# First product of each feed-forward by seven products of quarters instead of eight, and rms with positions on partitions

## Chip, cores and metric

The kernel runs on one core of one Trainium2 chip. What is measured is the device time of one execution in microseconds (us); several executions are timed and the median is given. One more execution is taken with the hardware profiler, and all rows below come from it. The core's engines each have a queue of their own, worked off in order: TensorE (PE; its weight loads PEld), VectorE (DVE), ScalarE (ACT), GpSimd (POOL), and SyncE (SP), which here issues the transfers. Matmuls write into eight accumulator banks (PSUM); all other tiles lie in the on-chip memory SBUF.

## The reference

A decoder trunk of two layers, 512 positions, width 1024, in float32. Layer 0 mixes by an RWKV recurrence, layer 1 by dilated attention, both with attention to a memory of 256 rows beside it. Ahead of and behind each mixer stands a feed-forward at half weight, so there are four: 00, 01, 10, 11.

```python
def swiglu_ffn(x, norm_g, w_in, w_out):
    gate, up = jnp.split(rms_norm(x, norm_g) @ w_in, 2, axis=-1)
    return (jax.nn.silu(gate) * up) @ w_out
...
        x = x + 0.5 * swiglu_ffn(x, ffn_pre_norm[layer], ffn_pre_w_in[layer], ffn_pre_w_out[layer])
```

`w_in` is 1024 x 5632 (2816 columns of gate, 2816 of up), `w_out` 2816 x 1024.

## The kernel before

Activations are kept transposed: features on the 128 partitions, the 512 positions along the free axis, so a state is 8 tiles of 128x512. Products run in a rounded float32 format (`fp32r`) with both factors split into a high part and the rest, and three matmuls for each 128x128 weight tile: high by high, high by low, low by high (`dense`). A weight comes in pieces of up to four tiles (128x512, 256 KB). For each piece `weight` issues the transfer into `raw` on SyncE's queue, copies it to the high part `whi` on ScalarE, and subtracts for the low part `wlo` on VectorE or GpSimd in turn. There are six `raw` slots and four each of `whi` and `wlo`.

In `ffn`, the operand u (parts `uh`, `ul`) is the state by the gain; the factor 1/rms (`rstd`) is applied after the product, since it belongs to the position. For each of the 22 column blocks m, the gate and the up product (8 tiles of k, 24 matmuls of 512 columns each) fill two of the eight banks `fps`. VectorE takes the gate by rstd (`gs`), ScalarE makes the Silu, VectorE multiplies it by up (`hm`), and this is split into `hh` on ScalarE and `hl` on VectorE. The second product goes over the 22 hidden blocks for each of the 8 output blocks j; `add_state` adds it to the old state, which is fetched again (`xin`), and forms the next operand.

Operand.rstd sums the squares over partitions with a matrix of ones, 128x512 wide, and takes root and reciprocal of all 128x512 equal rows. The memory's operand, the bias rows of the dilated attention (`bias_rows`, by way of DRAM) and the reload of the state for the shared keys and values run as side steps within the first products; the memory's keys and values (`memory_kv`) come behind 00, and within 01 at its last column block.

The order on each engine is made by the framework's scheduler from the order of the code; the slots of the pools (`take`) set when a tile can be filled again. All operations of the engines are recorded by one helper and so show line L278 in the profile; groups are told apart by tile names.

## Time and profile before

| | |
|---|---|
| three timed executions | 2134.22, 2135.74, 2138.95 us; median 2135.74 |
| profiled execution | 2133.36 us |
| its span, first to last instruction | 2131.6 us |
| mean granted TensorE clock | 0.995 of full speed |

By stage, in us from the start of the span: feed-forward 00 from 6 to 373, the memory's keys and values 373 to 386, first mixer to 805, feed-forward 01 to 1185, feed-forward 10 to 1546, second mixer to 1766, feed-forward 11 to the end. Of these, by busy time:

| stage | length | TensorE | VectorE | ScalarE | GpSimd |
|---|---|---|---|---|---|
| feed-forward 00 | 367 | 364.42 | 141.71 | 140.42 | 86.71 |
| first mixer | 419 | 379.59 | 270.42 | 159.86 | 150.80 |
| feed-forward 01 | 380 | 379.81 | 155.46 | 142.04 | 94.28 |
| feed-forward 10 | 361 | 360.59 | 131.78 | 128.89 | 86.61 |
| second mixer | 220 | 208.46 | 155.00 | 118.42 | 66.82 |
| feed-forward 11 | 365 | 359.52 | 120.83 | 116.69 | 89.24 |

A row of the profile that stands for a group gives engine, operation, written tile <- read tiles, shapes, the count, then busy time in us and the mean of one in ns, and behind it the idle time of its engine just before these instructions, with what ended it. A row of the timeline gives start and duration in us of a single instruction (x2: two of them run together).

### The profile page before, as it was taken

To read this page: it belongs to the slowest core of one execution; us is meant where nothing else is said; L and a number is where in the kernel's file an instruction comes from. 1 tells how busy PE (TensorE), PEld (TensorE's weight loads), DVE (VectorE), ACT (ScalarE), POOL (GpSimd) and SP (SyncE) were. 2 spreads that over 40 slices of the span, in tenths; PEclk is the share of its full clock that TensorE was granted. 3 is DMA by queue.
4 is the path that set the end of the run, shared out by engine and by line. 5 is a ranking of instruction groups with operands and counts; after the bars stand their busy time and mean duration, and the time that the engine had idled before them with its cause. 6 is when DMAs were issued, how large, how long until landed. Compare 5 with 4: busy or idle time off the path is not lost.

```text
span 2131.6 us, 32197 instructions
## 1 busy us (share of the span) xinstructions
PE 2065.4 (97%) x12734; PEld 1651.9 (77%) x12734; DVE 983.3 (46%) x1354; ACT 817.6 (38%) x1408; POOL 583.1 (27%) x502
## 2 busy tenths in 40 slices
PE   8999999979989899999999999999999999999999
PEld 6888888857666577778888888888877667888887
DVE  6333343575767747333434533324376675333322
ACT  6333333423333545333433433333345654333321
POOL 2222222643332133222222222222242224222221
PEclk9999999999999999999999999999999999999999
DMA  5322344311100045253344423234441144222342
GB/s 194 97 97 96 92 136 126 117 46 34 34 27 24 24 152 188 93 183 99 109 127 126 158 95 98 95 94 135 125 136 50 38 161 156 96 97 96 94 136 82
DMA packets 130632, 221.90 MB, mean 104 GB/s; under 512 B 14232, under 2 KB 31824, under 8 KB 130480
## 3 DMA queue, kind: packets, MB, share of 16 engines
q1 hardware_dynamic: 130480, 219.83, 32.8%
q8 instruction: 100, 1.64, 0.3%
q14 instruction: 52, 0.43, 0.1%
HBM read 202.89 MB, written 21.61 MB: 105 GB/s over the span
## 4 chain that ended last, share of the span: by engine, by line
PE 62%; DVE 2%; ACT 1%; issue 1%; DMA 0%; POOL 0%; SPq 0%; POOLq 0%; ACTq 0%; DVEq 0%
PE fps L278 50%; PE mm L278 6%; PE sc L278 4%; PE py L278 1%; DMA xin<-xd 0%; DVE prob L278 0%; DVE x L278 0%; DVE tmp L278 0%; DVE ul L278 0%; ACT krv L278 0%; DVE wlo L278 0%; DVE dmx L278 0%; POOL wlo L278 0%; DVE mpr L278 0%; ACT tmp L278 0%
## 5 line engine op out<-in xcount | busy, mean ns | idle before, releaser
L278 POOL TENSOR_TENSOR wlo<-raw,whi 128x512 fp32r<-128x512 f32 (+3 forms) x404 | 496.3, 1230 | 1439.7 <-ACT whi L278 1395.2
L278 ACT ACTIVATE whi<-raw 128x512 fp32r<-128x512 f32 (+3 forms) x684 | 416.1, 610 | 955.1 <-PE fps L278 778.7
L278 PE MATMUL fps<-uh,whi 128*128 128x512 f32 x1408 | 551.9, 392 | 7.6 <-ACT whi L278 7.6
L278 PE MATMUL fps<-uh,wlo 128*128 128x512 f32 x1408 | 550.0, 391 | 4.0 <-DVE wlo L278 2.4
L278 PE MATMUL fps<-ul,whi 128*128 128x512 f32 x1408 | 549.2, 390 | 0.0
L278 DVE TENSOR_TENSOR wlo<-raw,whi 128x512 fp32r<-128x512 f32 x280 | 201.2, 719 | 347.0 <-ACT whi L278 337.3
L278 PEld LDWEIGHTS fps<-uh,whi 128*128 128x128 f32 x1408 | 264.9, 188 | 68.3 <-ACT whi L278 11.1
L278 PEld LDWEIGHTS fps<-uh,wlo 128*128 128x128 f32 x1408 | 264.9, 188 | 62.0 <-DVE wlo L278 4.1
L278 PEld LDWEIGHTS fps<-ul,whi 128*128 128x128 f32 x1408 | 265.0, 188 | 56.0 <-issue 0.7
L278 PE MATMUL fps<-hh,whi 128*128 128x512 f32 x704 | 273.9, 389 | 0.0
L278 PE MATMUL fps<-hl,whi 128*128 128x512 f32 x704 | 273.9, 389 | 0.0
L278 PE MATMUL fps<-hh,wlo 128*128 128x512 f32 x704 | 273.9, 389 | 0.0
L278 DVE TENSOR_TENSOR gs<-fps,rstd 128x512 f32<-128x512 f32 x88 | 60.5, 690 | 322.9 <-PE fps L278 322.9
L278 PEld LDWEIGHTS fps<-hh,whi 128*128 128x128 f32 x704 | 132.1, 188 | 27.5
L278 PEld LDWEIGHTS fps<-hh,wlo 128*128 128x128 f32 x704 | 132.1, 188 | 27.4
L278 PEld LDWEIGHTS fps<-hl,whi 128*128 128x128 f32 x704 | 132.1, 188 | 27.4
L278 PE MATMUL mm<-uh,whi 128*128 128x512 f32 x280 | 120.6, 431 | 1.3 <-DVE x L278 0.9
L278 DVE TENSOR_TENSOR hm<-fps,gs 128x512 f32<-128x512 f32 x88 | 60.6, 691 | 121.5 <-PE fps L278 115.8
L278 PE MATMUL mm<-ul,whi 128*128 128x512 f32 x280 | 114.7, 410 | 1.1 <-DVE ul L278 1.1
L278 PE MATMUL mm<-uh,wlo 128*128 128x512 f32 x280 | 113.3, 405 | 0.0
L278 DVE RECIPROCAL tmp<-tmp 128x128 f32<-128x128 f32 x112 | 97.8, 918 | 29.1 <-ACT tmp L278 29.0
L278 DVE TENSOR_TENSOR hl<-hm,hh 128x512 fp32r<-128x512 f32 x88 | 76.9, 877 | 50.7 <-ACT hh L278 50.7
(256 smaller groups left out, 2115.5 us busy)
## 6 DMA issues: line engine op xcount, KB each, us to landing
raw<-w SPq DMA_DIRECT2D x512, 256.0 KB, 2.7
raw<-wa_in SPq DMA_DIRECT2D x44, 256.0 KB, 3.0
xd<-x SPq DMA_DIRECT2D x40, 256.0 KB, 3.8
tmp<-xd SPq DMA_DIRECT2D x32, 256.0 KB, 3.7
xin<-xd SPq DMA_DIRECT2D x32, 256.0 KB, 4.2
raw<-w_kv SPq DMA_DIRECT2D x24, 256.0 KB, 2.8
raw<-w SPq DMA_DIRECT2D x32, 128.0 KB, 2.3
raw<-wmem SPq DMA_DIRECT2D x16, 256.0 KB, 2.6
```

What stands on the lines that cost most here:

```text
L278: r = f(*args, **kw)
```

## The change

**The products.** Column blocks 0 and 1 are still computed whole. The other 20 are taken in ten pairs p = 1 to 10 of neighbouring blocks. For one block, gate and up form the two rows of a 2x2 matrix of weight quarters whose columns are the even and the odd tiles of k (the weights are laid out so on the host): quarters 11 and 12 of gate, 21 and 22 of up, each of four tiles. The operand has two halves of k and two halves of 256 positions. Seven products of quarters (numbered 1 to 7, each 4 x 3 matmuls of 256 columns) take the place of eight: 1 uses quarter 11, 2 quarter 12, 4 quarter 22, and 5, 6, 7, 3 use the sums S1 = 21 + 22, S2 = S1 - 11, S3 = 11 - 21, S4 = 12 - S2. The sums are formed on GpSimd in float32 and then split like weights. Sums of operand quarters stand beside them: t1 is made in Operand.add in the second half of the even parts; t2, t3, t4 are made in each feed-forward by `turns`, which fetches the state again. Of a pair's three banks, X holds 1 and 2, Y holds 6, 7 and 4, Z holds 5 and 3; VectorE adds what is taken from them (`g` tiles s1, s2, s3).

**The order.** On TensorE it is written out: 6(p), 1(p+1), 7(p), 2(p), 4(p), 5(p+1), 3(p). Low parts of weights are on VectorE in the first product, but those of product 4 are on GpSimd. Low parts of the hidden blocks are on GpSimd; the low parts of the weights of the second product are all on VectorE.

**The rest.** The rms is worked out in a column per 128 positions (128x4) and spread again by a matmul. The memory's operand, keys and values and the bias rows (in nine pieces of 256) are side steps of the second product; the reload for the shared keys and values stands in the second mixer. At the start the state comes in the order 0, 2, 4, 6, 1, 3, 5, 7.

```diff
@@ class Operand @@
+        if self.turns and j % 2 == 0:
+            d = net.xp.tile([P, TH], F32, tag="turn", bufs=1, name=net.nm("turn"))
+            net.split_into(h[:, :TH], l[:, :TH], x[:, :TH], gain)
+            nc.vector.tensor_tensor(d, x[:, TH:], x[:, :TH], op=ALU.subtract)
+            net.split_into(h[:, TH:], l[:, TH:], d, gain)
...
+    def column(self, ps):
...
+        for b in range(n // P):
+            nc.tensor.matmul(ps[:, b:b + 1], self.acc[:, b * P:(b + 1) * P], net.ones[:, :1], start=True, stop=True,
+                             skip_group_check=True)
...
+        nc.scalar.activation(c, ps, AF.Sqrt, bias=net.eps, scale=1.0 / D)
+        nc.vector.reciprocal(c, c)
...
-        nc.tensor.matmul(ps[:, :n], net.ones, self.acc, start=True, stop=True)
+    def spread(self, c, ps):
...
+            nc.tensor.matmul(ps[:, b * P:(b + 1) * P], c[:, b:b + 1].broadcast_to([P, P]), net.ident, start=True,
+                             stop=True, skip_group_check=True)
...
-        nc.scalar.activation(r, ps[:, :n], AF.Sqrt, bias=net.eps, scale=1.0 / D)
-        nc.vector.reciprocal(r, r)
+        nc.scalar.activation(r, ps[:, :n], AF.Copy)
@@ class Net @@
-        eng = nc.vector if self.split % 2 and not self.busy_vector else nc.gpsimd
+        eng = nc.vector if self.busy_gpsimd or self.split % 2 and not self.busy_vector else nc.gpsimd
...
+    def plus(self, out, a, b, op=ALU.add):
+
+        self.turn = (self.turn + 1) % 3
+        (self.nc.vector if self.turn else self.nc.gpsimd).tensor_tensor(out, a, b, op=op)
...
+    def both(self, raw, eng=None):
...
+        self.nc.scalar.activation(hi, raw, AF.Copy)
+        (eng or self.nc.vector).tensor_tensor(lo, raw, hi.bitcast(F32), op=ALU.subtract)
...
+    def product(self, ps, w, movs, first):
+
+        hi, lo = w
+        for k, (xh, xl) in enumerate(movs):
+            for a, b in ((hi, xh), (hi, xl), (lo, xh)):
+                self.nc.tensor.matmul(ps, a[:, k], b, start=first, stop=False, skip_group_check=True)
+                first = False
...
+    def turns(self, xin, gain, place, room):
...
+        for i in range(KD // 2):
+            a, b = (room(i, q).rearrange("p (s u) -> p s u", s=2) for q in range(2))
+            for q, x in enumerate((a, b)):
+                nc.sync.dma_start(x, xin[:, 2 * i + q].rearrange("p (s u) -> p s u", s=2))
+            g = self.v(gain, 2 * i + 1)
+            act.activation(a, a, AF.Copy, scale=self.v(gain, 2 * i))
+            vec.scalar_tensor_tensor(b[:, 1], b[:, 1], g, a[:, 1], op0=ALU.mult, op1=ALU.subtract)
+            vec.tensor_tensor(a[:, 0], b[:, 1], a[:, 0], op=ALU.add)
+            vec.scalar_tensor_tensor(b[:, 0], b[:, 0], g, a[:, 0], op0=ALU.mult, op1=ALU.subtract)
...
@@ def ffn @@
+                def sums(q):
+                    at = [S[:, (self.eighth + i) % 8] for i in range(3)]
+                    self.eighth += 3
+                    s1, s2, s3 = at
+                    gp.tensor_tensor(s1, q.raw("21"), q.raw("22"), op=ALU.add)
+                    gp.tensor_tensor(s2, s1, q.raw("11"), op=sub)
+                    gp.tensor_tensor(s3, q.raw("11"), q.raw("21"), op=sub)
...
+                    gp.tensor_tensor(s4, q.raw("12"), q.have["S2"], op=sub)
...
+            form = {1: ("11", b11), 2: ("12", b21), 3: ("S4", b22), 5: ("S1", t1)}
...
+                X, Y, Z = banks[p]
+                d = tiles[p]
+                ps = {1: X, 2: X, 6: Y, 7: Y, 4: Y, 5: Z, 3: Z}[n]
...
+                    w = self.both(q.have[name] if name[0] == "S" else q.raw(name), gp if n == 4 else vec)
+                    self.product(ps[:, i], w, movs, n in (1, 5, 6) and i == 0)
+                if n == 1:
+                    d["s1"] = tile_g()
+                    act.activation(d["s1"], X, AF.Copy)
+                elif n == 6:
+                    d["s2"] = tile_g()
+                    vec.tensor_tensor(d["s2"], Y, d["s1"], op=ALU.add)
+                elif n == 7:
+                    d["s3"] = tile_g()
+                    vec.tensor_tensor(d["s3"], Y, d["s1"], op=ALU.add)
+                    vec.tensor_tensor(d["s3"], Z, d["s3"], op=ALU.add)
+                elif n == 2:
+                    g = d["g"] = tile_g()
+                    vec.tensor_tensor(g, X, rs[0], op=ALU.mult)
+                    act.activation(g, g, AF.Silu)
+                elif n == 4:
+                    vec.tensor_tensor(d["s1"], Y, d["s1"], op=ALU.add)
+                    vec.tensor_tensor(raw_h[p][:, :, :TH], d["s1"], d["g"], op=ALU.mult)
+                elif n == 3:
+                    g = d["s2"]
+                    vec.tensor_tensor(g, Z, g, op=ALU.add)
+                    vec.tensor_tensor(g, g, rs[1], op=ALU.mult)
+                    act.activation(g, g, AF.Silu)
+                    vec.tensor_tensor(raw_h[p][:, :, TH:], d["s3"], g, op=ALU.mult)
...
+            with tc.high_priority(offset=150):
+                for n, ps in enumerate(whole):
+                    act.activation(early[n // 2][:, n % 2], ps[:, :TH], AF.Copy)
+                odd = [self.both(w) for w in odd]
+            t2, t3, t4 = self.turns(xin, f"g{which}", (tp, tags, slots), lambda i, q: raw_h[NF // 2 - 1 - i][:, q])
+            form.update({4: ("22", t4), 6: ("S2", t2), 7: ("S3", t3)})
...
+            order = [(n, p) if n > 0 else (-n, p + 1) for p in range(1, NF // 2) for n in (6, -1, 7, 2, 4, -5, 3)]
...
+            for n, p in order:
+                step(n, p)
+                if p > 2 and n == 4:
+                    split_hidden()
...
+            self.busy_gpsimd = True
+            while len(hh) < NF:
+                split_hidden()
...
-                run(self.dense([(ps, w2[j])], h))
+                for _ in self.dense([(ps, w2[j])], hh):
+                    next(side, None)
@@ def trunk @@
-            net.ready = [net.weight(ap[f"w1_{which}"][m][:, :WB]) for m in (0, NF, 1, NF + 1)]
+            net.ready = net.lead(which)
...
-            net.ffn(ap["xT"], "00", op, [nxt], xd[0], before=[before], after=after)
+            net.ffn(ap["xT"], "00", op, [nxt], xd[0], second=steps)
...
-                rkv = net.ffn(xd[2], "10", op, [nxt], xd[3], before=[lambda p, bank: net.reload(ukv, xd[2])])
+                rkv = net.ffn(xd[2], "10", op, [nxt], xd[3], place=(pool, ("kvh", "kvl"), KD))
```

What this does to the queues is seen around pair p = 2 in feed-forward 00. On GpSimd, before, among the column blocks (`raw` a fetched weight, `whi` its high part):

```order
L278 TENSOR_TENSOR wlo_86_373<-raw_84_370,whi_85_372 128x512
L278 TENSOR_TENSOR wlo_92_409<-raw_90_406,whi_91_408 128x512
L278 TENSOR_TENSOR wlo_108_465<-raw_106_462,whi_107_464 128x512
L278 TENSOR_TENSOR wlo_114_501<-raw_112_498,whi_113_500 128x512
L278 TENSOR_TENSOR wlo_130_557<-raw_128_554,whi_129_556 128x512
```

Now, from S1 of pair 4 to S2 of pair 4 (`raw_230` and `raw_231` are quarters 21 of pair 4, `raw_205` and `raw_208` its 11, `raw_217` and `raw_218` the 12 of pair 3; S holds the sums and quarters 22; the two rows that write `wlo` are product 4 of pair 3):

```order
L309 TENSOR_TENSOR S_64_224<-raw_230_1240,S_64_224 128x512
L309 TENSOR_TENSOR S_64_224<-raw_217_1161,S_64_224 128x512
L309 TENSOR_TENSOR S_64_224<-raw_218_1164,S_64_224 128x512
L309 TENSOR_TENSOR S_64_224<-S_64_224,raw_205_1088 128x512
L309 TENSOR_TENSOR S_64_224<-raw_205_1088,raw_230_1240 128x512
L309 TENSOR_TENSOR S_64_224<-raw_208_1106,raw_231_1246 128x512
L309 TENSOR_TENSOR wlo_225_1203<-S_64_224,whi_224_1202 128x512
L309 TENSOR_TENSOR wlo_227_1219<-S_64_224,whi_226_1218 128x512
L309 TENSOR_TENSOR S_64_224<-raw_231_1246,S_64_224 128x512
L309 TENSOR_TENSOR S_64_224<-S_64_224,raw_208_1106 128x512
```

Where GpSimd had one low part for two weights, it has a row of ten operations for a pair of blocks, in which the second S1 stands behind the low parts of product 4.

On VectorE, before, one column block (`gs` and `hm` read the banks):

```order
L278 TENSOR_TENSOR wlo_327_1414<-raw_325_1411,whi_326_1413 128x512
L278 TENSOR_TENSOR gs_319_1400<-fps_305_1326,rstd_66_321 128x512
L278 TENSOR_TENSOR wlo_333_1450<-raw_331_1447,whi_332_1449 128x512
L278 TENSOR_TENSOR hm_320_1403<-fps_306_1327,gs_319_1400 128x512
L278 TENSOR_TENSOR hl_322_1406<-hm_320_1403,hh_321_1405 128x512
```

Now, from the end of product 4 of pair 2 to the operation that frees bank Y of pair 3 (`g_129` is s1, `g_160` what is taken of bank Z, `h_55` the hidden blocks of pair 2, `g_201` the s2 of pair 3, `fps_162` its bank Y):

```order
L309 TENSOR_TENSOR g_129_594<-fps_121_556,g_129_594 128x512
L309 TENSOR_TENSOR wlo_196_1032<-S_64_224,whi_195_1031 128x512
L309 TENSOR_TENSOR h_55_215<-g_129_594,g_182_934 128x2x256
L309 TENSOR_TENSOR wlo_198_1052<-S_64_224,whi_197_1051 128x512
L309 TENSOR_TENSOR wlo_200_1068<-S_64_224,whi_199_1067 128x512
L309 TENSOR_TENSOR wlo_207_1091<-raw_205_1088,whi_206_1090 128x512
L309 TENSOR_TENSOR g_160_818<-fps_122_557,g_160_818 128x512
L309 TENSOR_TENSOR wlo_210_1109<-raw_208_1106,whi_209_1108 128x512
L309 TENSOR_TENSOR g_160_818<-g_160_818,rstd_98_411 128x512
L309 TENSOR_TENSOR wlo_213_1127<-S_64_224,whi_212_1126 128x512
L309 TENSOR_TENSOR h_55_215<-g_175_893,g_160_818 128x2x256
L309 TENSOR_TENSOR g_201_1083<-fps_162_821,g_170_859 128x512
```

Between two takings of a bank now stand low parts of four different products, and s2 comes last of them.

More of the change, by code (lines that the diff above doesn't have):

```diff
@@ L19 @@
 T = 512
+TH = T // 2
 D = 1024
@@ new lines, in ffn @@
+            whole = [bank().rearrange("p s u -> p (s u)") for _ in range(4)]
+            early = [tile_g() for _ in range(2)]
+            mine = [w1[m + i * NF] for m in range(2) for i in range(2)]
+            begun = self.ready or self.lead(which)
+            self.ready = ()
+            odd = [self.raw(w[:, WB:]) for w in mine]
+            for k in range(0, KD, 2):
+                for ps, w in zip(whole, begun):
+                    self.product(ps, [t[:, k // 2:k // 2 + 1] for t in w], [u.parts[k]], k == 0)
@@ new lines, in ffn @@
+            with tc.high_priority(offset=150):
[4 more added lines that the diff above has]
+            form.update({4: ("22", t4), 6: ("S2", t2), 7: ("S3", t3)})
+            for n, ps in enumerate(whole):
+                self.product(ps, odd[n], [u.parts[k] for k in range(1, KD, 2)], False)
+                e = early[n // 2][:, n % 2]
+                vec.tensor_tensor(e, ps[:, TH:], e, op=ALU.add)
+                if n == 0:
+                    column = u.column(extra())
+                elif n == 2:
+                    r = u.spread(column, extra())
@@ L501, in memory_operand @@
             yield FREE
-        to.append(u.rstd(bank("sc")))
+        c = u.column(bank("sc"))
+        for _ in range(8):
+            yield FREE
+        to.append(u.spread(c, bank("sc")))
+        yield FREE
     def memory_kv(self, layer, tmp, bank, operand, out):
@@ L995, in reload, with bias_rows @@
             yield FREE
-    def bias_rows(self, rows, dst, pool, bank):
+    def bias_rows(self, rows, dst, pool, tmp, bank):
         nc = self.nc
@@ L1212, in after @@
-            def after(pool, bank):
-                return net.memory_kv(layer, tmp(pool), bank, operand, out)
-            return pool, out, before, after
+                    if j % 2 == 0:
+                        tiles[j] = [net.xp.tile([P, 2, MEM], F32R, tag=t, bufs=KD, name=net.nm(t)) for t in ("uh", "ul")]
+                    return tuple(t[:, j % 2] for t in tiles[j - j % 2])
+                yield from net.memory_operand(layer, tmp, bank, place, operand)
+                yield from net.memory_kv(layer, tmp, bank, operand, out)
```

270 lines of the change are left out of this document (183 added, 87 removed).

## Prediction

> **What bounds the kernel now.** I read the summary of the page first, then its chain that ended last.
>
> ```profile
> span 2131.6 us, 32197 instructions
> PE 2065.4 (97%) x12734; PEld 1651.9 (77%) x12734; DVE 983.3 (46%) x1354; ACT 817.6 (38%) x1408; POOL 583.1 (27%) x502
> ...
> PEclk9999999999999999999999999999999999999999
> ...
> PE fps L278 50%; PE mm L278 6%; PE sc L278 4%; PE py L278 1%; DMA xin<-xd 0%; DVE prob L278 0%; DVE x L278 0%; DVE tmp L278 0%; DVE ul L278 0%; ACT krv L278 0%; DVE wlo L278 0%; DVE dmx L278 0%; POOL wlo L278 0%; DVE mpr L278 0%; ACT tmp L2
> ```
>
> TensorE works in 97% of the span at a full clock, and half of the chain is matmuls into `fps`, the banks of the feed-forwards. Whether a stage has idle time in it is read from the windows, here the middle of the second and of the fourth feed-forward (columns: window, its length, then busy time and count by engine).
>
> ```profile
> 824.00:1041.00 217.00, 217.00 (x942) 174.66 (x941) 85.18 (x118) 82.83 (x134) 50.64 (x39) 1.00 0.37 120
> 1790.00:2110.00 320.00, 320.00 (x1413) 264.92 (x1413) 106.18 (x139) 104.27 (x167) 74.69 (x61) 1.00 0.34 106
> ```
>
> TensorE has no idle microsecond in either; VectorE is busy for 39% of the first, GpSimd for 23%. So the bound is the matmuls' own pace, and the starts of single matmuls give it: the first and last of a run of 512 columns, then of 256 (the products of the memory's keys and values).
>
> ```profile
> 899.76 0.39 PE L278 MATMUL fps<-uh,whi 128*128 128x512 f32 x1
> ...
> 903.84 0.39 PE L278 MATMUL fps<-uh,whi 128*128 128x512 f32 x1
> ...
> 373.21 0.28 PE L278 MATMUL fps<-mh,whi 128*128 128x256 f32 x1
> ...
> 384.61 0.28 PE L278 MATMUL fps<-mh,wlo 128*128 128x256 f32 x1
> ```
>
> Eighteen steps in 4.08 us are 0.2267 us for 512 columns; 95 steps in 11.40 us are 0.1200 us for 256.
>
> **What the change takes away.** Of the 22 column blocks of gate and up, two are computed as before and 20, taken in ten pairs, by seven products. A block cost 2 x 8 x 3 = 48 matmuls of 512 columns, 48 x 0.2267 = 10.88 us. Now it costs 7 x 4 x 3 = 84 of 256 columns, 84 x 0.1200 = 10.08 us. That is -0.80 us a block, -16.0 us in a feed-forward and **-64 us** in four. An eighth fewer products would be worth 1.36 us a block; the narrower matmuls, at 0.1200 instead of 0.1134, give 0.56 of it back.
>
> The page "TensorE: Matmul & The Clock Gate" of the Trainium skill, section "Back-to-back issue gap", gives the isolated gap as N/2.4 + 2.5 ns; worked out from that page as an estimate it would be 215.8 and 109.2 ns, and -95 us in place of -64. The rows above are 5% and 10% over it, so the measurement stands.
>
> **What it adds, and where.** Per pair of blocks (14 weights, 20.16 us of matmuls) GpSimd now forms eight sums of quarters and the low parts of product 4; VectorE forms the other twelve low parts, six operations that read a bank, and three more from SBUF only (the product with r and the two halves of h). Before, each engine split every second weight.
>
> ```profile
> L278 POOL TENSOR_TENSOR wlo<-raw,whi 128x512 fp32r<-128x512 f32 (+3 forms) x404 | 496.3, 1230 | 1439.7 <-ACT whi L278 1395.2
> L278 ACT ACTIVATE whi<-raw 128x512 fp32r<-128x512 f32 (+3 forms) x684 | 416.1, 610 | 955.1 <-PE fps L278 778.7
> L278 DVE TENSOR_TENSOR wlo<-raw,whi 128x512 fp32r<-128x512 f32 x280 | 201.2, 719 | 347.0 <-ACT whi L278 337.3
> L278 DVE TENSOR_TENSOR gs<-fps,rstd 128x512 f32<-128x512 f32 x88 | 60.5, 690 | 322.9 <-PE fps L278 322.9
> ```
>
> ScalarE has 14 high parts, a copy, two Silus and up to two hidden splits: 19 x 0.610 = 11.6 us in 20.16, no bound. By these means GpSimd has 10 x 1.23 = 12.3 us and VectorE 15 x 0.72 + 6 x 0.69 = 14.9, so each alone would be hidden. Together they are not, and the end of the second mixer shows why (first GpSimd, then VectorE).
>
> ```profile
> 1761.82 1.30 POOL L278 TENSOR_TENSOR sq<-sq,sq 128x512 f32<-128x512 f32 x1
> 1763.22 1.59 POOL L278 TENSOR_TENSOR wlo<-raw,whi 128x512 fp32r<-128x512 f32 x1
> 1764.78 3.45 POOL L278 TENSOR_TENSOR sq<-sq,sq 128x512 f32<-128x512 f32 x2
> ...
> 1761.79 1.88 DVE L278 SCALAR_TENSOR_TENSOR ul<-qn,vec,uh 128x512 fp32r<-128x512 f32 x1
> 1763.59 1.77 DVE L278 TENSOR_TENSOR wlo<-raw,whi 128x512 fp32r<-128x512 f32 x1
> 1765.29 1.77 DVE L278 SCALAR_TENSOR_TENSOR ul<-qn,vec,uh 128x512 fp32r<-128x512 f32 x1
> ```
>
> With both queues full the operations go strictly by turns. GpSimd ends at 1763.12 and 1764.81, VectorE at 1763.67 and 1765.36: after each end of GpSimd's, VectorE needs 0.55 us, then GpSimd 1.14. A cycle of 1.70 us holds one of each; neither makes way in the middle. A lone meeting in a feed-forward says the same (GpSimd, then VectorE).
>
> ```profile
> 1066.11 1.30 POOL L278 TENSOR_TENSOR wlo<-raw,whi 128x512 fp32r<-128x512 f32 x1 [4.15 <-ACT whi L278]
> ...
> 1065.65 0.69 DVE L278 TENSOR_TENSOR hm<-fps,gs 128x512 f32<-128x512 f32 x1 [1.50 <-PE fps L278]
> 1067.04 0.92 DVE L278 TENSOR_TENSOR hl<-hm,hh 128x512 fp32r<-128x512 f32 x1 [0.70 <-ACT hh L278]
> ```
>
> `hl`, with both inputs in SBUF, ends 0.55 us after GpSimd does; `hm`, which reads a bank, overlaps GpSimd's row by 0.23 and both keep their length. I take 1.16 us of the shared way for an operation of GpSimd and 0.55 for one of VectorE's with two SBUF inputs. Then a pair holds it for 10 x 1.16 + 15 x 0.55 = 19.85 us of 20.16.
>
> The Trainium skill speaks against this change in "SBUF — State Buffer", section "SBUF: two separate sides": GpSimd and a VectorE instruction with two SBUF inputs take the port pair as an exclusive lock, and whoever comes second waits for the whole instruction. By that rule the sums of quarters hold it like the splits. The rows above agree for splits and squares; no run here yet shows a sum of two raw tiles on GpSimd.
>
> **What of it lies on the path.** Each pair has one tight place. Product 7 of the next pair may start only once `s2` has been taken out of the bank Y that 6, 7 and 4 share. From the end of product 4, TensorE has 5, 3, 6 and 1 to do: 8 x 1.44 = 11.52 us of cover. In that time VectorE's queue holds s1, a low part, half of h, three low parts, g from Z, a low part, g times r, a low part, the other half of h, then s2: nine with two SBUF inputs and three from banks, 9 x 0.60 (0.55 with its start) + 3 x 0.69 = 7.5 us, behind a full bank. GpSimd's queue has S1, two S4, S2 and S3 for that stretch: if each gets in between, 5 x 1.16 = 5.8 us more, 13.3 us in all, **1.8 us over the cover**. Besides, s1 stands behind low parts of product 5, which wait for the second S1, which waits for quarter 22, which is fetched into S only after product 7 has freed its slot and GpSimd has done its two low parts.
>
> ```profile
> raw<-w SPq DMA_DIRECT2D x512, 256.0 KB, 2.7
> ...
> xin<-xd SPq DMA_DIRECT2D x32, 256.0 KB, 4.2
> ```
>
> From the end of 7 that is two low parts (2.3), the transfer (2.7), S1 (1.2), its high part (0.6) and its low part (0.6): 7.4 us. Product 4 ends 5.76 us after 7, so s1 can be 1.6 us late. Nothing before shows this chain, so I bound it: 0 if GpSimd's operations fall where VectorE waits anyway; 1.8 + 1.6 = 3.4, rounded up by one hold to 4.6, at the other end. I take **3.2 us**, near the plain sum, because the shared way is 98% full and leaves few gaps. The last pair has no successor: 9 x 3.2 = 28.8 us a feed-forward, +115 in four.
>
> **Hidden splits.** GpSimd also gets ten hidden low parts inside the loop, standing between the sums. 0 to 10 x 1.16 = 11.6 us; I take 9, since each pushes back sums that the tight place waits for: **+36** in four. The others come at the start of the second product, where only one weight is split per 2.7 us of matmuls: nothing.
>
> **The start of a feed-forward.** Between the even and the odd k, ScalarE splits four weights before or amid four copies of banks, and VectorE has the row of reloaded turns to form.
>
> ```profile
> L278 DVE SCALAR_TENSOR_TENSOR ul<-x,vec,uh 128x512 fp32r<-128x512 f32 x9 | 6.7, 750 | 5.5 <-ACT uh L278 5.5
> ```
>
> The eight reloads land in 4.2 us beside 48 x 0.2267 = 10.9 us of matmuls. Of four groups of three VectorE operations (0.75 each, 9 us) and the first evictions most is covered; 1 to 6 us stick out, I take 3.3: **+13**.
>
> **The rest.** The rms by positions removes this from the way of the first eviction, but TensorE runs on meanwhile in both kernels: nothing.
>
> ```profile
> L278 DVE RECIPROCAL rstd<-rstd 128x512 f32<-128x512 f32 x1 | 3.3, 3340 | 0.0
> ```
>
> The bias rows now go through the second product of 01 in nine steps. Each matmul stands 6 others (1.36 us) behind its transfer, in TensorE's own order.
>
> ```profile
> hot<-hot SPq DMA_DIRECT2D x2, 64.0 KB, 1.8
> ```
>
> That is 9 x 0.44 = 4 us at least if nothing covers, 9 x 1.36 = 12 if a full step is lost each time, 0 if the buffers run ahead; **+6**. The memory's head norms, moved among the second products, wait similarly for small chains: **+2**. Before the first product four weights instead of two are fetched and split: **+2**. The reload in the second mixer comes 16 us before its use: 0.
>
> **Sum.** -64 + 115 + 36 + 13 + 6 + 2 + 2 = +110 us. The profiled execution took 2133.36 us, 1.8 over its span; 2133.4 + 110 = **2243 us**. That execution was 2.4 us under the median of the runs.
>
> **Rivals.**
> The tight place is wide enough. If no more than three of GpSimd's five operations get between (3.5 us into the 11.52 - 7.5 = 4.0 that are spare) and S1 is in time, TensorE keeps its 20.16 us: 2133.4 - 64 + 23 = 2092 us, **faster**. For it speaks that both engines' work just fits; against it that 19.85 of 20.16 are taken. Chance 0.12.
> The shared way is used without gaps, and alone sets the time. For 10 pairs and 14 hidden parts it is 114 x 1.16 + 150 x 0.55 = 214.7 us, in place of 20 x 10.88 = 217.6: -3 us each, 2133.4 - 12 + 23 = 2144 us. Chance 0.13; it needs every wait of one queue for the other to be filled by a third operation.
> The late quarter 22 and the tight place add up in full and feed each other, 4.6 to 6 us a pair: at 5.4, 9 x 5.4 x 4 = 194, 2133.4 - 64 + 194 + 36 + 23 = 2322 us. Chance 0.15.
> That the products are not cheaper at all (weights that load no faster than 0.120 us) is excluded by the run of 95 steps, which has a new weight at each.
>
> **Chances and range.** My forecast 0.60, the others as above. A measurement here tells 0.2% from no change. Faster holds the first rival and a little of the second: 0.14; same 0.03; slower 0.83. The range leaves out the first rival and the far end of the third: 2138 to 2330.
>
> **What would show it.** VectorE's `wlo` would rise from 0.72 to over 1.2 us in the loop, GpSimd's sums would stand at 1.2 to 1.7, and TensorE would be idle before product 7 (`fps<-th`), released by VectorE's `g`, for about 3 us a pair, with 234 us for ten pairs. If `wlo` keeps 0.7 while sums run on GpSimd, the lock does not hold for them; if TensorE is busy throughout, the first rival is right; if it waits before product 5 for GpSimd's S1 or a transfer, the third.

## The result, and the profile after

The changed kernel takes 2323.51 us (median of 4 runs, 2319.75 to 2325.88) against 2136.17 us for the kernel before (4 runs, 2134.22 to 2138.95): 1.0874 times as long, 95% interval 1.0854 to 1.0895. It is slower, by 187 us where 110 were forecast; the time lies inside the range, near the rival with the longer chain (2322 us).

First the summary of the changed kernel's profile and its chain.

```profile
span 2320.0 us, 40107 instructions
PE 2084.3 (90%) x15718; PEld 1778.4 (77%) x15718; DVE 1621.9 (70%) x2044; ACT 975.2 (42%) x1770; POOL 972.4 (42%) x720
...
PE 40%; DVE 14%; issue 5%; DMA 4%; ACT 2%; POOL 1%; SPq 0%; DVEq 0%; ACTq 0%; POOLq 0%
```

TensorE's share of the span fell from 97% to 90%, and VectorE's busy time rose from 983 to 1622 us, with 690 more instructions. The windows of the ten pairs in feed-forwards 00, 10 and 11 (columns as before the change) show where.

```profile
34.00:294.00 260.00, 215.10 (x1680) 208.31 (x1678) 221.95 (x238) 116.39 (x210) 168.54 (x115) 0.95 0.27 83
...
1313.50:1561.00 247.50, 215.12 (x1682) 208.66 (x1681) 205.07 (x213) 107.90 (x188) 163.09 (x112) 0.97 0.26 80
...
1942.50:2192.00 249.50, 214.52 (x1680) 206.65 (x1680) 207.54 (x218) 107.29 (x188) 162.35 (x110) 0.97 0.26 80
```

1680 matmuls of 256 columns at 0.120 us are 201.6 us; the stages take 247 to 260. TensorE is idle for 32 to 45 us of each, and its granted clock (the first number behind GpSimd's busy time) is 0.95 to 0.97. The groups name what was stretched and who was waited for.

```profile
L309 DVE TENSOR_TENSOR wlo<-S,whi 128x512 fp32r<-128x512 f32 x320 | 331.0, 1053 | 117.8 <-ACT whi L309 117.8
L309 DVE TENSOR_TENSOR h<-g,g 128x512 f32<-128x512 f32 x80 | 132.6, 1657 | 4.3 <-ACT g L309 1.4
...
L309 POOL TENSOR_TENSOR S<-raw,S 128x512 f32<-128x512 f32 x160 | 240.3, 1518 | 138.2 <-DMA S<-w 72.7 <-DMA raw<-w 36.6 <-DVE wlo L309 25.5
...
L309 PE MATMUL fps<-th,whi 128*128 128x256 f32 (+1 forms) x888 | 279.0, 314 | 65.5 <-DVE g L309 62.2 <-ACT whi L309 3.3
```

VectorE's low parts of sums take 1053 ns and its last product for a hidden block 1657, both with two inputs in SBUF; a low part took 719 before. And TensorE stood 62 us ahead of matmuls on reloaded turns (`th`, in 00, 01 and 11) until VectorE's `g` was done: the wait for bank Y. The timeline ahead of product 7 of pair 4 in feed-forward 10, where the turns stand in tiles called `kvh` and `kvl`, shows it in one place (GpSimd, VectorE, TensorE).

```profile
1391.55 1.72 POOL L309 TENSOR_TENSOR h<-h,hh 128x512 fp32r<-128x512 f32 x1
1393.22 1.74 POOL L309 TENSOR_TENSOR S<-raw,S 128x512 f32<-128x512 f32 x1
1394.92 1.73 POOL L309 TENSOR_TENSOR h<-h,hh 128x512 fp32r<-128x512 f32 x1
1396.62 1.75 POOL L309 TENSOR_TENSOR S<-S,raw 128x512 f32<-128x512 f32 x1
...
1390.36 1.78 DVE L309 TENSOR_TENSOR h<-g,g 128x512 f32<-128x512 f32 x1
1392.06 3.45 DVE L309 TENSOR_TENSOR wlo<-S,whi 128x512 fp32r<-128x512 f32 x2
1395.43 1.77 DVE L309 TENSOR_TENSOR wlo<-raw,whi 128x512 fp32r<-128x512 f32 x1
...
1401.93 0.68 DVE L309 TENSOR_TENSOR g<-fps,g 128x512 f32<-128x512 f32 x1
...
1402.75 0.36 PE L309 MATMUL fps<-kvh,whi 128*128 128x256 f32 x1 [2.33 <-DVE g L309]
```

From 1390 to 1397 the two engines go by turns with a cycle of 1.70 us, the one of the mixer's rows before. The hidden low parts (`h<-h,hh`) stand between GpSimd's sums. At the end of the row stands s2, and TensorE waits 2.33 us for it. The same row also begins late (GpSimd, VectorE).

```profile
1384.70 1.29 POOL L309 TENSOR_TENSOR S<-raw,S 128x512 f32<-128x512 f32 x1 [2.06 <-DMA S<-w]
...
1386.69 1.83 DVE L309 TENSOR_TENSOR wlo<-S,whi 128x512 fp32r<-128x512 f32 x2 [2.75 <-ACT whi L309]
1388.44 0.68 DVE L309 TENSOR_TENSOR g<-fps,g 128x512 f32<-128x512 f32 x1
```

GpSimd waits 2.06 us for quarter 22 to land, VectorE stands idle for 2.75 us until the high part of the S1 formed from it is there, and s1 (at 1388.44) stands behind that low part. From there to the end of s2 VectorE has no gap of over 0.1 us. The mean over the first eight pairs of all four feed-forwards: s1 begins 2.2 us after the last matmul of product 4 (0.35 in the first run below, where nothing holds it up), and from its start to the end of s2 it takes 13.6 us.

What follows on the wait is new: the windows around it, and two matmuls behind it.

```profile
1380.00:1400.00 20.00, 18.41 (x145) 17.40 (x144) 16.40 (x17) 6.96 (x12) 15.00 (x10) 1.00 0.25 80
1400.00:1402.70 2.70, 0.42 (x4) 0.22 (x2) 2.60 (x4) 1.36 (x4) 1.27 (x1) 1.00 0.06 11
1402.70:1406.00 3.30, 3.25 (x18) 3.28 (x19) 2.48 (x3) 2.64 (x5) 1.59 (x2) 0.61 0.44 150
...
1403.63 0.42 PE L309 MATMUL fps<-kvh,whi 128*128 128x256 f32 x1
1403.85 0.42 PE L309 MATMUL fps<-kvl,whi 128*128 128x256 f32 x1
```

Over the 3.3 us after the wait the mean granted clock is 0.61, and from 1403.4 on the matmuls start 0.21 us apart instead of 0.12.

The 187 us by stage, from the starts of matmuls in both traces:

| part, four feed-forwards together | predicted | measured |
|---|---|---|
| matmuls, at 0.2267 and 0.1200 us | -64 | -64 |
| product 7 of pair 1 to product 7 of pair 10, over the matmuls' pace | +115 + 36 | +171 |
| from there to the second product | 0 | +9 |
| whole blocks and first pair, less what those stages lost before | +13 + 2 | +38 |
| second products with side steps | +6 + 2 | +30 |
| mixers | 0 | +3 |

The side steps that now stand in the second products stood in the first ones before. What they cost there is part of the 22 us that the line of the starts takes off, and counts again in the line of the second products; these two lines are firm only together, +68 where 23 were taken.

### The profile page after: what moved, and what is told of

Its sections match the earlier page's. It is cut to its first block, busy times and chain, and to the rows that moved or that the text cites. A ratio compares the mean times of both kernels' runs of the same rounds, so it can differ in the third digit from the quotient of the medians.

```text
span 2320.0 us, 40107 instructions
## 1 busy us (share of the span) xinstructions
PE 2084.3 (90%) x15718; PEld 1778.4 (77%) x15718; DVE 1621.9 (70%) x2044; ACT 975.2 (42%) x1770; POOL 972.4 (42%) x720
## 4 chain that ended last, share of the span: by engine, by line
PE 40%; DVE 14%; issue 5%; DMA 4%; ACT 2%; POOL 1%; SPq 0%; DVEq 0%; ACTq 0%; POOLq 0%
PE fps L309 30%; DVE wlo L309 6%; PE mm L309 5%; PE sc L309 3%; DVE g L309 3%; DVE h L309 3%; DMA S<-w 2%; PE py L309 1%; ACT whi L309 1%; PE ex L309 1%; DMA xin<-xd 1%; POOL wlo L309 1%; ACT g L309 1%; DMA raw<-w 1%; DVE ul L309 1%
## 5 line engine op out<-in xcount | busy, mean ns | idle before, releaser
L309 DVE TENSOR_TENSOR wlo<-raw,whi 128x512 fp32r<-128x512 f32 (+1 forms) x400 | 363.1, 920 | 243.2 <-ACT whi L309 241.0
L309 PE MATMUL fps<-uh,wlo 128*128 128x256 f32 (+1 forms) x1408 | 422.5, 300 | 33.7 <-DVE wlo L309 33.4
L309 PE MATMUL fps<-uh,whi 128*128 128x256 f32 (+1 forms) x1408 | 418.0, 297 | 19.6 <-ACT whi L309 7.2
L309 PE MATMUL fps<-ul,whi 128*128 128x256 f32 (+1 forms) x1408 | 415.5, 295 | 0.1
L309 DVE TENSOR_TENSOR wlo<-S,whi 128x512 fp32r<-128x512 f32 x320 | 331.0, 1053 | 117.8 <-ACT whi L309 117.8
L309 POOL TENSOR_TENSOR wlo<-raw,whi 128x512 fp32r<-128x512 f32 (+3 forms) x124 | 149.5, 1210 | 555.3 <-ACT whi L309 517.8
L309 PE MATMUL fps<-th,whi 128*128 128x256 f32 (+1 forms) x888 | 279.0, 314 | 65.5 <-DVE g L309 62.2
L309 PE MATMUL fps<-th,wlo 128*128 128x256 f32 (+1 forms) x888 | 279.1, 314 | 30.9 <-DVE wlo L309 30.8
L309 PE MATMUL fps<-h,whi 128*128 128x512 f32 x704 | 278.7, 396 | 0.0
L309 PE MATMUL fps<-tl,whi 128*128 128x256 f32 (+1 forms) x888 | 276.5, 311 | 0.0
```

Of the source, the lines that this page charges most:

```text
L309: r = f(*args, **kw)
```

## The experiments

Theory A is that of the prediction: operations of VectorE and GpSimd on SBUF tiles wait out each other, and this stretches VectorE's row to the tight place. Theory B is the rival in which the transfers, above all the late quarter 22, and the order of the queues set the pace. Runs one to four, six, seven and ten were executed once; the four executions of the changed kernel lie within 6.1 us.

**First run, the sums left out.**

```diff
-                    gp.tensor_tensor(s1, q.raw("21"), q.raw("22"), op=ALU.add)
-                    gp.tensor_tensor(s2, s1, q.raw("11"), op=sub)
-                    gp.tensor_tensor(s3, q.raw("11"), q.raw("21"), op=sub)
-                    q.have.update(S1=s1, S2=s2, S3=s3)
+                    q.raw("21")
+                    s1 = q.raw("22")
+                    q.have.update(S1=s1, S2=s1, S3=s1)
...
-                    gp.tensor_tensor(s4, q.raw("12"), q.have["S2"], op=sub)
+                    q.raw("12")
+                    q.have["S4"] = q.have["S1"]
```

> The eight sums of quarters a pair are left out: products 5, 6, 7 and 3 take quarter 22 in place of the sums, so the output is another one; transfers, splits, matmuls and evictions stay. Theory A (VectorE's operations on two SBUF tiles wait out whole operations of GpSimd): two of GpSimd's ten operations a pair are left, the pair's period falls from 23.6 to 20.2-20.8 us, VectorE's low parts to about 0.7 us, and the start of each feed-forward is some 5 us shorter: 2323 - 4 x (31 + 5) = about 2180 us, and down to 2135 if the hidden low parts are hidden too. Theory B (transfers and the order of the queues set the pace): the period stays over 22.5 us, 2280 us or more.

Measured: 2132.63 us. Product 7 follows on product 7 of the pair before after 20.0 to 20.1 us, with two hidden low parts in some pairs, so these are hidden too. Where six stand in one pair it is 20.9, and at the first pair of 00 22.0; the last pair has another order. It is the lower of the two figures of theory A. VectorE's low parts and its last product:

```profile
L309 DVE TENSOR_TENSOR wlo<-S,whi 128x512 fp32r<-128x512 f32 x320 | 249.6, 782 | 70.0 <-ACT whi L309 63.8
...
L309 DVE TENSOR_TENSOR h<-g,g 128x512 f32<-128x512 f32 x80 | 66.3, 829 | 1.9 <-ACT g L309 1.4
```

They fall from 1053 to 782 and from 1657 to 829 ns though VectorE does the same work. Without a single sum the kernel is still no faster than the kernel before (2134.79 us measured beside it): what the matmuls save is spent at the starts, in the second products and in smaller losses. (It also has more slots for quarter 22, so by itself it doesn't exclude theory B.)

**Second run, the sums on VectorE.** In the four lines of the sums `vec.tensor_tensor` takes the place of `gp.tensor_tensor`.

```diff
-                    gp.tensor_tensor(s1, q.raw("21"), q.raw("22"), op=ALU.add)
+                    vec.tensor_tensor(s1, q.raw("21"), q.raw("22"), op=ALU.add)
...
```

> The same sums, formed by VectorE. Theory A: VectorE then has 23 x 0.60 + 6 x 0.69 = 17.9 us a pair and meets only the two low parts of product 4 on GpSimd (2.3 us), 20.2 of 20.16 us: period 21 to 22 us, 2323 - 4 x (9 x 2.1 + 5) = about 2225 us. Theory B: quarter 22 lands no earlier, and now VectorE's whole row waits for it: no gain, 2320 us or more.

Measured: 2182.00 us, 141 us less than the changed kernel, with eight more operations a pair on VectorE and the transfers as they were. Theory B by itself is out: it said no gain. The gain is larger than theory A's figure of 98. The period is 20.1 to 21.5 us without hidden low parts and 25.2 where six of them run on GpSimd. Quarter 22 is as late as it was: s1 begins 2.9 us after product 4. But from s1 to the end of s2 it now takes 9.8 us instead of 13.6, and TensorE's wait before product 7 falls from 2.3 to 0.9 us.

**Third run, only the hidden low parts on VectorE.**

```diff
-                gp.tensor_tensor(self.low[:, m % 2], x, h.bitcast(F32), op=sub)
+                vec.tensor_tensor(self.low[:, m % 2], x, h.bitcast(F32), op=sub)
```

> The low parts of the hidden blocks on VectorE instead of GpSimd. Theory A: ten of them in the loop hold the shared way for 0.55 instead of 1.16 us, 6 us a feed-forward, 2323 - 24 = about 2299 us, and the long periods (25.6 to 27.8 us) fall by 0.6 us for each hidden part. If they cost only by their place in GpSimd's row, the whole 11.6 us go: 2277 us. If VectorE's row is the tight one, nothing is gained: 2320 us.

Measured: 2312.24 us, 11 us less. The loop gains 2.6 to 5.6 us a feed-forward, less than the 6 expected. The openings of the second products lose part of it: that of 00 with its side steps goes from 135.3 to 137.8 us, that of 01 from 151.0 to 154.1.

**Fourth run, everything in the loop on VectorE.** The edits of the second and third runs, and:

```diff
-                    w = self.both(q.have[name] if name[0] == "S" else q.raw(name), gp if n == 4 else vec)
+                    w = self.both(q.have[name] if name[0] == "S" else q.raw(name), vec)
```

> Sums, the low parts of product 4 and the hidden low parts all on VectorE; GpSimd has nothing in the loop. Theory A: 25 x 0.60 + 6 x 0.69 = 19.1 us a pair without any wait for GpSimd, and 0.8 on the mean for hidden parts: 20.0 of 20.16 us, so a period of 20.5 to 21.5: about 2180 us. Theory B: 2320 us or more, since VectorE waits for the transfers in its row.

Measured: 2171.29 us. The pairs of feed-forward 10, the groups of low parts and of the last product:

```profile
1239.80:1445.00 205.20, 202.41 (x1681) 200.87 (x1679) 195.61 (x323) 110.31 (x189) 0.00 (x0) 1.00 0.30 95
...
L309 DVE TENSOR_TENSOR wlo<-S,whi 128x512 fp32r<-128x512 f32 x400 | 272.5, 689 | 4.2 <-ACT whi L309 1.9
...
L309 DVE TENSOR_TENSOR h<-g,g 128x512 f32<-128x512 f32 x80 | 55.1, 689 | 0.0
```

VectorE still waits for quarter 22 before it forms S1, 37.7 us in all four feed-forwards:

```profile
L309 DVE TENSOR_TENSOR S<-raw,S 128x512 f32<-128x512 f32 x160 | 110.5, 697 | 38.3 <-DMA S<-w 37.7
```

GpSimd has nothing to do; VectorE, with ten more operations a pair than in the changed kernel, is busy for less time (195.6 against 205.1 us), since each takes its own 0.69 us. It works 95% of the stage and TensorE loses 3.6 us in 205. So what filled VectorE's row was waiting, not work. The second products pay, since the hidden low parts at their opening now stand on VectorE too: 141.5, 159.4, 127.6 and 126.6 us against 135.3, 151.0, 122.7 and 123.2.

**Fifth run, the other half of the change by itself:** the kernel before with the rms in a column of 128x4 and spread again.

```diff
-        nc.tensor.matmul(ps[:, :n], net.ones, self.acc, start=True, stop=True)
+        for b in range(n // P):
+            nc.tensor.matmul(ps[:, b:b + 1], self.acc[:, b * P:(b + 1) * P], net.ones[:, :1], start=True, stop=True,
+                             skip_group_check=True)
...
+        for b in range(n // P):
+            nc.tensor.matmul(ps[:, b * P:(b + 1) * P], c[:, b:b + 1].broadcast_to([P, P]), net.ident, start=True,
+                             stop=True, skip_group_check=True)
```

> The kernel before with nothing changed but the rms: the column of 128x4 and its spread take the place of the 128x512 root and reciprocal. My step: VectorE's 3.3 us stand beside matmuls in either form, so no change: 2136 us, within 0.2%. Rival: the reciprocal delays the first evictions and so a bank: 4 x 1 to 3 us faster. Other rival: eight more small matmuls and a chain over four engines on TensorE's row: 4 x 1 to 2 us slower.

Measured: 2151.69 us, 1.0065 times the kernel before (1.0042 to 1.0089): slower, and more so than the rival said. Two things are seen. The first is a round trip in TensorE's row, here the memory's rms in feed-forward 01.

```profile
833.53 0.40 PE L285 MATMUL fps<-uh,whi 128*128 128x512 f32 x1
836.09 2.08 PE L285 MATMUL fps<-cst,rcol 128*128 128x128 f32 x8 [2.16 <-DVE rcol L285]
...
839.24 0.63 PE L285 MATMUL fps<-ul,whi 128*128 128x512 f32 x1
839.67 0.63 PE L285 MATMUL fps<-uh,wlo 128*128 128x512 f32 x1
...
833.50:843.00 9.50, 7.34 (x25) 5.82 (x24) 6.05 (x9) 5.29 (x9) 1.84 (x2) 0.64 0.32 110
```

TensorE waits 2.16 us for the column, and for the next 3 to 4 us its matmuls are 0.43 us apart; the clock over the window is 0.64. The first product of 01 is 7.5 us longer. In the changed kernel other products stand between column and spread in the feed-forwards, so this wait is not in it (0.9 us, once); the 0.65% are therefore not the price of this half there. The second thing: all four second products take 121.03 us instead of 119.84, without a gap. The second mixer is 3 us longer in this execution; why is open.

**Sixth and seventh runs**, on the changed kernel: the bias rows copied out by 12 transfers instead of 36, and the four leading low parts on GpSimd.

```diff
-            for _ in range(n):
-                nc.sync.dma_start(dst[:, h % 4, v * 256:(v + 1) * 256],
-                                  rows[h:h + 1, v * 256:(v + 1) * 256].broadcast_to([P, 256]))
-                v += 1
-                yield FREE
+            nc.sync.dma_start(dst[:, h % 4, v * 256:(v + n) * 256],
+                              rows[h:h + 1, v * 256:(v + n) * 256].broadcast_to([P, n * 256]))
+            yield FREE
```

```diff
-        return [self.both(self.raw(w1[m + i * NF][:, :WB])) for m in range(2) for i in range(2)]
+        return [self.both(self.raw(w1[m + i * NF][:, :WB]), self.nc.gpsimd) for m in range(2) for i in range(2)]
```

> The changed kernel, with the bias rows copied out by 12 transfers (four of seven pieces) instead of 36 of one piece each. Theory: in the second product of 01 the weights' transfers stand behind these issues in SyncE's row (0.6 to 0.7 us each); 24 fewer free 16 us of it, and the second product with its side steps falls from 151.0 to about 140 us: 2312 us. Rival: the waits come from the small products and their round trip through DRAM, not from the issues: 2322 us.

> The changed kernel, with the low parts of the four leading weights on GpSimd instead of VectorE. Theory for the start: behind the mixers these low parts stand in VectorE's row behind the next operand's parts, which alternate with GpSimd's squares; ahead of the squares on GpSimd they are early. Whole blocks of 01 from 31.3 to 26 us, of 11 from 36.3 to 27: 2323 - 14 = 2309 us. Rival: TensorE waits for the operand itself, whoever splits: 2322 us or, with slower GpSimd, a few more.

Measured: 2319.40 and 2323.39 us: both theories miss, and the rivals' 2322 us fit within the spread. With 12 transfers the second product of 01 falls only from 151.0 to 148.5 us, with the early low parts the whole blocks of 11 go from 36.3 to 37.3. What happens to the bias is seen in the changed kernel (the queue of SyncE, then ScalarE):

```profile
1221.22 4.40 SPq L1265 DMA_DIRECT2D bdram<-rdram  x6
...
1231.19 0.63 ACT L309 ACTIVATE whi<-raw 128x512 fp32r<-128x512 f32 x1 [9.61 <-DMA raw<-w]
```

Copies stand in a row on the queue that fetches weights, and ScalarE is idle 9.6 us for a weight. TensorE waits 2.4 us of that, and 4.7 us in the whole stage, for high parts of weights. Fewer but larger copies still stand in one row ahead of the weights (eleven in 9.62 us in the eighth run).

**Eighth run, the edits together:** the second run's, the loop's low parts on VectorE, those at the opening of the second product on GpSimd, and the edits of the sixth and seventh.

```diff
-                gp.tensor_tensor(self.low[:, m % 2], x, h.bitcast(F32), op=sub)
+                (gp if self.busy_gpsimd else vec).tensor_tensor(self.low[:, m % 2], x, h.bitcast(F32), op=sub)
```

> Sums, product 4's low parts and the loop's hidden low parts on VectorE as in the fourth run, but the hidden low parts that open the second product on GpSimd (second products of 10 and 11 from 127 back to 123 us), with the twelve bias transfers and the leading low parts on GpSimd. If the gains add up: 2171 - 4 x 5 - 11 - 14 = about 2126 us, a little under the kernel before; if start and bias gains are not there, about 2150.

Measured: 2161.29 us, 1.0112 times the kernel before (1.0086 to 1.0138). The second products of 10 and 11 are back at 122.7 and 123.2 us; start and bias gained little.

**Ninth run, where tiles stand.**

```diff
-        c = net.xp.tile([P, T // P], F32, tag="rcol", bufs=2, name=net.nm("rcol"))[:, :n // P]
+        c = net.xp.tile([P, 64], F32, tag="rcol", bufs=2, name=net.nm("rcol"))[:, :n // P]
```

> The fifth run again, its 128x4 column in slots of 256 bytes a partition instead of 16, so that what is allocated behind it moves by 512 bytes instead of 64; no operation differs. Theory of place: in the fifth run the second products take 121.03 us without a gap where the kernel before takes 119.84, since their tiles stand 64 bytes on; with 512 they go back to 119.84, 4 x 1.2 us and some in the mixers less, about 2146 us. Theory of the round trip: the rest stays, above all TensorE's wait of 2.55 us for the column in feed-forward 01 and the slower matmuls behind it (about 7 us). If place explains nothing: 2151 us and 121.03; if everything: 2137.

Measured: 2151.81 us, 1.0067 (1.0039 to 1.0096), no gain in all. But the second products are at 119.84 us again, to the hundredth. The group of the last second product in the fifth run, then in this one:

```profile
L285 PE MATMUL fps<-hh,whi 128*128 128x512 f32 x176 | 69.3, 394 | 0.0
...
L285 PE MATMUL fps<-hh,whi 128*128 128x512 f32 x176 | 68.5, 389 | 0.0
```

So 64 bytes in the place of the tiles cost 1% of the matmuls' pace in the second products; this is shown. That it makes the kernel faster is not: the 4.8 us given back are gone elsewhere in the profiled execution, which was the slowest of its five (both mixers together 5 us longer, the first product of 00 4); why is open.

**Tenth run, the start of a feed-forward off GpSimd:** the sums of the first pair, the low parts of the reloaded turns, and the squares behind the mixers on VectorE.

```diff
-        (self.nc.vector if self.turn else self.nc.gpsimd).tensor_tensor(out, a, b, op=op)
+        self.nc.vector.tensor_tensor(out, a, b, op=op)
...
-                    gp.tensor_tensor(s1, q.raw("21"), q.raw("22"), op=ALU.add)
+                    (vec if q.m < 4 else gp).tensor_tensor(s1, q.raw("21"), q.raw("22"), op=ALU.add)
...
-            op, nxt = nxt, Operand(net, "g01", sums="gpsimd", later=True, turns=True)
+            op, nxt = nxt, Operand(net, "g01", later=True, turns=True)
```

> The changed kernel, with what GpSimd does at the start of a feed-forward moved to VectorE: the sums of the first pair, a third of the low parts of the reloaded turns, the squares behind the mixers. Theory: the start's 60 us over the matmuls' pace (whole blocks 27.5, 31.3, 24.1, 36.3 for 21.8 each, then 24.3, 18.6, 15.2, 15.9 for 11.5 each up to product 7 of the first pair) are for the most part VectorE waiting by turns with GpSimd; some 28 of them go: 2295 us. Rival: the start waits for transfers and for the operand's parts: 2318 us or more.

Measured: 2312.76 us, 11 us less. Whole blocks and first pair together fall from 51.8, 49.9, 39.3, 52.2 to 47.1, 43.9, 35.7 and 46.6 us: 20 of the expected 28. Which of the three moves did it is not separated. The mixers were 14 us longer in this execution, which the eleventh run, with the same edit, doesn't show; that is open. In the changed kernel the start of feed-forward 00 reads so (VectorE, then TensorE):

```profile
38.01 4.29 DVE L309 TENSOR_TENSOR tl<-h,th 128x512 fp32r<-128x512 f32 x3
...
45.04 0.68 DVE L309 TENSOR_TENSOR wlo<-raw,whi 128x512 fp32r<-128x512 f32 x1
...
45.77 0.58 PE L309 MATMUL fps<-uh,wlo 128*128 128x256 f32 x1 [10.03 <-DVE wlo L309]
```

Three low parts of turns take 4.29 us, 1.4 each, while GpSimd forms the first pair's sums; TensorE waits 10 us for a low part that stands behind the turns and the first evictions.

**Eleventh run, all that helped:** the eighth's without leading low parts on GpSimd, with the tenth's, bias rows in the second product of 10 and eight steps apart, part of the opening low parts on VectorE, and the 128x4 column in the slot of another tile, so that all tiles stand as in the kernel before.

```diff
-        c = net.xp.tile([P, T // P], F32, tag="rcol", bufs=2, name=net.nm("rcol"))[:, :n // P]
+        c = net.xp.tile([P, TH], F32, tag="turn", bufs=1, name=net.nm("rcol"))[:, :n // P]
...
+            for _ in range(8):
+                yield FREE
...
-                rkv = net.ffn(xd[2], "10", op, [nxt], xd[3], place=(pool, ("kvh", "kvl"), KD))
+                rkv = net.ffn(xd[2], "10", op, [nxt], xd[3], place=(pool, ("kvh", "kvl"), KD),
+                              second=lambda tmp, bank: net.bias_rows(rdram, bdram, p, tmp, bank))
```

> All of the loop and the start on VectorE, only the last hidden low parts at the opening of the second product on GpSimd; the bias rows in the second product of 10 with twelve copies set eight steps apart; the column of 128x4 in a slot that is there already, so that all tiles stand as in the kernel before. If place costs what the traces say (second products 122.7 instead of 119.8) and start and bias gains add up: 2161 - 12 - 12 - 10 = about 2127 us, 0.4% under the kernel before. If the start doesn't mend: 2140 us.

Measured: 2146.83 us (10 runs), 1.0038 times the kernel before (1.0018 to 1.0058), above both figures. The second product of 11 is at 120.1 us, as place said; the other three take 139.3, 140.2 and 127.0 us, with part of the opening low parts on VectorE and the bias rows in that of 10. No version of mine is faster than the kernel before.

## Why the prediction came out as it did

**The gain.** -64 us was right: without sums a pair takes 20.0 to 20.1 us where 20.16 was worked out.

**The tight place and the turns of the two engines.** Right in mechanism and in place: the cycle of 1.70 us, the wait of TensorE for s2, VectorE's low parts at 1.05 instead of 0.72 us (1.2 was named). Both parts of the plain sum are there: s1 late by 1.6 us was worked out and 2.2 are measured, the row to s2 13.3 against 13.6 (12.8 where no hidden low part stands in it), under a cover of 11.52. The second and fourth runs show that the turns set the length of the row: moving eight and then all ten operations a pair from GpSimd to VectorE, which adds work to the busier engine, shortened it to 9.8 and 9.6 us and took 141 and 152 us off the kernel. The Trainium skill, page "SBUF — State Buffer", section "SBUF: two separate sides", says that GpSimd and VectorE with two SBUF inputs exclude each other; these runs agree, now for sums of raw tiles too: VectorE's last product for a hidden block takes 1657 ns with the sums on GpSimd and 689 with GpSimd idle.

The loop lost 171 us where 151 were taken. The waits alone are about 136 us of it, less than the forecast. A hidden low part was priced too high: two of them lengthen the row to s2 by 1.5 us and six by 3.5, 6.5 in a feed-forward where 9 were taken, and taking them off GpSimd gave 2.6 to 5.6 (third run). TensorE's wait is split: some 2 us before product 7, over 1 us inside product 6, where the low part of the first weight is late, and 0.4 in 5.

The other 36 us were not in the sum: **the clock falls behind the longer waits**. From 20 us after the start on, the trace has the granted clock at half in 22 stretches of 3.41 us or a multiple of it, 106 us together; the kernel before has 5, of 20 us together. Of TensorE's waits of 1.4 to 2.0 us none of 54 runs into such a stretch, of those of 2.0 to 3.0 us 13 of 18 do, and of the longer ones all ten. In the kernel before two of nine waits of 1.4 to 2.0 us do, so no threshold is shown. Some 460 matmuls of 256 columns start 0.16 to 0.26 us apart, 43.6 us more than at 0.12; the kernel before has 52 such, 5.0 us. I priced waits at their own length and did not see that TensorE pays again after them. In the Trainium skill's "TensorE: Matmul & The Clock Gate", section "HAM oscillation — how this bites in real kernels", an idle gap over some 3.4 us brings this about; here waits of 2.1 to 2.7 us did.

The +9 us behind the last product 7 of the loop were taken at nothing; what they are is open.

**The start** is the term that was mis-sized most: +38 us where 15 were taken, outside the 1 to 6 a feed-forward that I gave as bounds. I costed VectorE's row of turns at its free durations and as covered, though I had just shown that operations beside GpSimd's take 1.7: the first pair's eight sums run beside that row. With the sums left out altogether (first run) the same line is +15, as it was taken, so they are what the term lacked; the tenth run, which moves those of the first pair with two other things to VectorE, gave 20 us.

**The second products**: +30 where 8 were taken. Of it the bias is the larger part: the second product of 01 is 19.6 us over its matmuls (151.0 against 131.4 with those of the memory's keys and values), that of 00, which has no bias, 3.9. I bounded the bias by waits on TensorE's row, 0 to 12 us. Of the 19.6 us, 4.7 are the eighteen bias products themselves, which stood in the first product before, 4.7 are waits for weights, behind copies on SyncE's queue, and 1.7 the half pace that follows on the longest of them. That these 36 issues share a queue with the weights was in the order, and I did not count them; but 24 fewer issues gave only 2.5 us (sixth run), so the issues alone don't explain it. In 10 and 11 the second product is 3 us slower without any gap: that is the place of tiles, which I did not think of and which holds in 00 and 01 too. The rest is open.

**The rms** as "nothing" holds in the feed-forwards, where products stand between its two halves; with the halves side by side it isn't nothing (fifth run), and the slots of its column move the tiles (ninth and eleventh runs).

**Rivals.** "The tight place is wide enough" fails as long as sums run on GpSimd, and is nearly true without (fourth run). "The shared way is used without gaps" fails too: the stages of the ten pairs take 247 to 260 us where it had 214.7. The third rival, the late quarter 22 and the tight place in full, is right that both add up, as the forecast had it too; the late quarter is a part of the loss, not the whole. The second and fourth runs leave it (s1 2.9 and 2.1 us late) and shorten the row, and the loop's loss falls from 171 to 46 and 21 us. What an earlier quarter 22 would save with the sums on GpSimd was not tried. That the rival's 2322 us is so near is luck: its loop would cost 194 + 36 = 230 us where 171 were measured, and the starts and second products, which it took no dearer than the forecast did, make up for that.

## What to carry to other kernels

Before work is put on an idle engine, ask whether it shares a way with the busy one: here ten operations a pair on GpSimd cost VectorE more time than doing them itself. A saved eighth of the matmuls must pay for what feeds them: at 20 us a pair there was room for 20 us of VectorE, and a wait of TensorE that grew from 1.7 to 2.5 us mostly cost another 1.5 us of half pace behind it. Look for what side work stands in front of on the queue that carries the weights; another queue for it was not tried here.

## What the runs showed of the hardware that I had not expected

Behind most waits of TensorE of 2.1 to 2.7 us and all longer ones the clock falls to half for 3.41 us or a multiple of it (mean granted clock 0.61 and 0.64 in windows around two of them, one in the changed kernel and one in the fifth run); behind 54 waits of 1.4 to 2.0 us in the changed kernel it didn't, in the kernel before behind two of nine it did.

Moving all tiles of the second product by 64 bytes slowed its matmuls of 512 columns by 1% (121.03 against 119.84 us); by 512 bytes it didn't. In the changed kernel, where they stand 64 or 128 bytes off, they take 122.7 to 123.2 us, and 120.1 when put back.
